# A two-layer hybrid decoder on one core: the query projections in another place in the order of work

## The chip, the core and the metric

The kernel runs on one core of a Trainium2 chip: TensorE (PE, matmuls), VectorE (DVE), ScalarE (ACT), GpSimd (POOL), and SyncE (SP), which issues all DMAs. The metric is the device time of one execution in microseconds (us); less is better.

## What is computed

Two layers over 512 prompt tokens and 64 sample tokens (8 sequences of 8) at width 1024. Each layer normalises the stream, projects it with one wide weight matrix, and runs two branches beside each other: retention (4 heads) and attention over the 128 (prompt) or 66 (sample) positions that an indexer scores highest. Both are gated, merged, projected out, and a gated per-layer input is added.

```python
def decoder_layer(x, p_i, pos, ret_s0, past, topk, ...):
    h = rmsnorm(x, g_norm)
    rq, rk, rv, rz, aq, ak, av, az, iq, ik, iw, gr, ga = in_projection(h, w_in, pos, q_gain, k_gain)
    o_r, s_new = retention(rq, rk, rv, ret_s0)
    u_r = einsum('bte,ed->btd', group_norm_heads(o_r) * silu(rz), w_o_ret)
    o_a = sparse_attention(aq, pos, k_all, v_all, iq, iw, ik_all, topk)
    u_a = einsum('bte,ed->btd', o_a * silu(az), w_o_att)
    m = sigmoid(gr) * u_r + sigmoid(ga) * u_a
    x = x + einsum('btd,de->bte', m, w_out)
    gate = sigmoid(einsum('btd,de->bte', x, w_ple_gate))
    return x + gate * einsum('btp,pd->btd', p_i, w_ple_proj), ak, av, ik, s_new
```

## The kernel before

Every float32 weight and activation is split into a high and a low part (`whi`/`wlo`, `xh`/`xl`), and each product is three matmuls (hi·hi, lo·hi, hi·lo). Weights arrive 1024 columns at a time in two staging buffers `wst`; `convert` makes the parts (ACT writes `whi`, DVE `wlo`).

The work is written as Python generators, one for each strand. A planner (`Streams.go`) keeps a model clock for each engine, estimates each operation's duration (`Op.dur`, by `_duration`), and issues next, again and again, the operation that could start first; priorities (`PRIO`) break ties. Its result is one fixed instruction order for each engine. On the chip each engine runs its own list strictly in order and waits where an operand is not there. Operations are all recorded by one helper, so the trace gives them all line L297; they are told apart by tiles.

The main strand of a layer walks through `PLAN`, a list of units, and issues their projections on PE. A unit of `proj_a` is 48 matmuls of 288 columns into PSUM banks `pm` (three of them); a unit of `proj_b` does five token tiles, 112 matmuls of 256 columns. Each finished bank is read out ("evacuated") by DVE and ACT:

- `kx`, `iq`: keys, values and indexer queries; `rv`: retention values; `az`: the attention branch's gate (`silz<-pm,R`).
- `aq0`, `aq1`: the attention queries, two groups of four heads (`aqx`). For each tile DVE scales (`misc<-pm,rcol,gqk`), normalises and rotates them in `misc` (three buffers `QQ`), PE transposes them (`ta<-cst,misc`), and ACT and DVE write them to `qs` (four slots `QS`; attention gives one back when it has finished a block and group).
- `rt h` stands for three units `rq`, `rk`, `rz` of retention head h, 0 to 3. `rq` and `rk` are rotated on the way out (`xl<-pm,rot`, `tb<-tb,rot`), `rz` is a gate (`silz<-pm,R`). Behind `rz` the strands `ret_p` (prompt) and `ret_s` (sample) of the head are started.
- `gr`, `ga` 0 to 7: 16 gate units (`misc<-pm,R`), spilled to DRAM.
- `wo`/`merge`, `wout`, `pp`, `wpg`: the output side. The first merge waits until all side strands have ended (`for e in sides`).

The side strands fill the engines beside the projections: `indexer` 1 to 3, one for each of the query blocks that need a selection (scores on PE, then 16 rounds of MAX8 and MATCH_REPLACE8 on DVE over 256, 384 and 512 columns of `xl`; lowest priority), `indexer_s`, `attend` (blocks j = 0 to 3, each with both query groups u, two key/value heads each, at most two pairs in flight), `attend_s`, `ret_p`, `ret_s`. Block j of `attend` waits for its indexer, and (j, u) for the queries of group u.

What sets the order here is the line `PLAN` and `Op.dur`:

```python
PLAN = _plan("kx iq rv0 rv1 az0 az1 az2 az3 aq0 aq1 rt0 rt1 rt2 rt3")
```

Of the kernel before, what the change touches and what calls it, by code (L numbers as in the profile page):

```python
# [105 lines left out]
class Op:  # L106
    __slots__ = ("eng", "fn", "a", "k", "name", "outs", "ins", "dur", "form")

    def __init__(self, eng, fn, name, a, k):
        self.eng, self.fn, self.name, self.a, self.k = eng, fn, name, a, k  # L110
        aps = [x for x in list(a) + list(k.values()) if isinstance(x, bass.AP)]
        out = k.get("out", a[0] if a else None)
        acc = k.get("accum_out")
        self.outs = [_box(x) for x in (out, acc) if x is not None]
        self.form = (_val(a[1].partition_size) > 64, min(2, _free(a[1]) - 1 >> 5)) if eng == "PE" else None
        self.ins = [_box(x) for x in aps if x is not out and x is not acc]
        self.dur = _duration(eng, name, out, aps, a, k)


def _val(x):  # L120
    return x() if callable(x) else x


def _box(ap):
    span = 1 + sum(s * (n - 1) for s, n in list(ap.ap)[1:])
    t = ap.tensor
    if ap.space in (bass.MemoryType.SB, PSUM):
        row = list(ap.ap)[0][0] or 1
        p0 = _val(ap.start_partition)
        c0 = ap.offset % row if row > 1 else 0  # L130
        return t.name, p0, p0 + _val(ap.partition_size), c0, c0 + span
    first = list(ap.ap)[0]
    return t.name, 0, 1, ap.offset, ap.offset + span + first[0] * (first[1] - 1)


def _free(ap):
    n = 1
    for s, c in list(ap.ap)[1:]:
        n *= c
    return n  # L140


def _duration(eng, name, out, aps, a, k):
    n = max(_free(x) for x in aps)
    psum = any(x.space == PSUM for x in aps[1:])
    if eng == "PE":
        if name == "transpose":
            return 0.110
        lhs = aps[1]
        if lhs.dtype == FT:  # L150
            if _free(lhs) <= 32:
                return 0.030 + n * 0.4e-3
            return 2 * max(0.11, n / 1.2e3 + 0.005)
        return max(0.108, (n + 32) / 2.4e3)
    if eng == "DVE":
        if name == "memset":
            return (n + 8) / 0.96e3
        ptr = sum(1 for x in aps[1:] if _free(x) == 1 and n > 4 and x.space != PSUM)
        if name in ("tensor_scalar", "tensor_copy") and not psum and all(x.dtype == FT for x in aps[:2]):
            return (n / 2 + 66) / 0.96e3 + 0.062 * min(ptr, 2)  # L160
        return (n + 64) / 0.96e3 + 0.062 * min(ptr, 2)
    if eng == "ACT":
        ptr = sum(1 for x in aps[1:] if _free(x) == 1 and n > 1)
        return (n + (61 if psum else 112)) / 1.2e3 + 0.093 * min(ptr, 2)
    if eng == "POOL":
        return 0.3 + (0.165 if k.get("op", a[-1]) == OP.pow else 0.0022) * n
    return {"page": 0.5, "gather": 0.74}.get(name, 0.47)
# [144 lines left out]
def tile_hybrid_decoder(ctx: ExitStack, tc: tile.TileContext, A, O):  # L312
# [96 lines left out]
    def plan(l):  # L409
# [6 lines left out]

        for st in PLAN:
            name, i = st[0], st[1:]
# [147 lines left out]
    def layer(l, xh, xl, kxb):  # L566
# [692 lines left out]
        la = None  # L1259
        for st in PLAN:  # L1260
            name, i = st[0], st[1:]
# [265 lines left out]
def _plan(order):  # L1527
    p = []
    for t in order.split():
        n, i = t[:2], t[2:]  # L1530
        p += [(n,)] if not i else [("rq", int(i)), ("rk", int(i)), ("rz", int(i))] if n == "rt" else [(n, int(i))]
    p += [(n, d) for d in range(KT) for n in ("gr", "ga")]
    for d in range(KT):
        p += [("wo", d), ("merge", d)]
    return p + [("wout", d) for d in range(KT)] + [("pp", 0), ("pp", 1)] + [("wpg", d) for d in range(KT)]


PLAN = _plan("kx iq rv0 rv1 az0 az1 az2 az3 aq0 aq1 rt0 rt1 rt2 rt3")
PAIRS_IN_FLIGHT = 2
PRIO = dict(convert=0, load=1, tables=6, indexer=7, indexer_s=3, attend=3, attend_s=5, ret_p=6, ret_s=4)  # L1540
NSLOT = dict(s4=3, qs=4, t2=5, pt=1, hi=3, lo=3)
# [82 lines left out]
```

## Time and profile before

| | us |
|---|---|
| median of 3 runs (lowest, highest) | 1159.26 (1154.34, 1162.0) |
| the profiled execution | 1155.49 |
| its span, first to last instruction | 1153.7 |

The profile is of one execution. PE's rows show a matmul's time in flight; matmuls overlap, so a busy PE is not a PE at its full rate. The stages below are cut where PE starts the first matmul of a unit: layer 0 has az at 77.0, aq0 at 103.8, rq0 at 153.1, rq2 at 203.8, gr0 at 280.7, the merge at 413.2; layer 1 has them at 646.1, 672.5, 720.6, 774.7, 850.8 and 983.5.

### The profile page before, as it was taken

The page shows a single profiled execution, that of the slowest core. Times are in us where ns is not written, and L with a number is a line of the kernel's source. Part 1 is how long each engine was busy: PE and PEld are TensorE (multiplying, and loading weights), DVE is VectorE, ACT ScalarE, POOL GpSimd, SP SyncE. Part 2 cuts the span into 40 slices and gives each one's busy share as a digit, 9 for nine tenths or more (in the row PEclk, how much of TensorE's full clock was granted, in tenths as well). Part 3 has the DMA queues.
Part 4 walks back from the last instruction along what each step waited for, and adds up shares of the span by engine and source line. Part 5 has one row for each costly group of instructions (what it writes and reads, how often), then busy time and mean ns, then how long its engine had stood idle before and what let it go on. Part 6 is the DMA issues. An engine that isn't in the chain of part 4 may idle for free.

```text
span 1153.7 us, 21594 instructions
## 1 busy us (share of the span) xinstructions
PE 1098.1 (95%) x8426; PEld 1058.7 (92%) x8426; DVE 764.6 (66%) x1979; ACT 525.7 (46%) x1116; POOL 57.3 (5%) x68
## 2 busy tenths in 40 slices
PE   8999789898999999999999996988999999999998
PEld 7989788797999999999999986987889999999998
DVE  6799999766654366443658999996576533764433
ACT  6732455554663343235446334565557533422331
POOL 0100110001000000000010011010000000000000
PEclk9999979999999999999999997998999999999999
DMA  6532112231333355523335111312323233655231
GB/s 194 153 113 74 37 55 83 86 115 53 97 107 115 125 192 157 184 87 109 105 113 168 63 56 37 111 38 94 113 74 107 88 114 125 203 168 163 80 122 47
DMA packets 53112, 124.80 MB, mean 108 GB/s; under 512 B 7442, under 2 KB 19602, under 8 KB 53010
## 3 DMA queue, kind: packets, MB, share of 16 engines
q1 hardware_dynamic: 53010, 123.42, 32.8%
q8 instruction: 66, 1.08, 0.4%
q14 instruction: 36, 0.29, 0.1%
HBM read 103.05 MB, written 20.35 MB: 107 GB/s over the span
## 4 chain that ended last, share of the span: by engine, by line
PE 65%; DVE 25%; ACT 4%; issue 3%; DMA 2%; SPq 1%; POOL 0%; DVEq 0%; ACTq 0%
PE pm L297 53%; DVE xl L297 7%; DVE sm L297 5%; DVE wlo L297 3%; PE acc L297 3%; PE oT L297 2%; PE tq L297 2%; PE tr L297 2%; DVE misc L297 2%; PE ta L297 2%; ACT tb L297 1%; DVE silz L297 1%; DVE t2k L297 1%; ACT whi L297 1%; DVE qs L297 1%
## 5 line engine op out<-in xcount | busy, mean ns | idle before, releaser
L297 PE MATMUL pm<-xh,whi 128*128 128x288 f32 x1536 | 460.0, 299 | 2.5 <-DVE misc L297 2.0
L297 PE MATMUL pm<-xh,wlo 128*128 128x288 f32 x1536 | 459.9, 299 | 0.0
L297 PE MATMUL pm<-xl,whi 128*128 128x288 f32 x1536 | 459.3, 299 | 0.0
L297 PEld LDWEIGHTS pm<-xh,whi 128*128 128x128 f32 x1536 | 292.0, 190 | 4.4 <-issue 1.8
L297 PEld LDWEIGHTS pm<-xl,whi 128*128 128x128 f32 x1536 | 292.3, 190 | 0.9 <-issue 0.4
L297 PEld LDWEIGHTS pm<-xh,wlo 128*128 128x128 f32 x1536 | 292.0, 190 | 1.1 <-issue 0.5
L297 ACT ACTIVATE whi<-wst 128x1024 fp32r<-128x1024 f32 (+4 forms) x148 | 150.1, 1016 | 218.3 <-PE pm L297 145.7
L297 DVE TENSOR_TENSOR wlo<-wst,whi 128x1024 fp32r<-128x1024 f32 (+4 forms) x148 | 173.0, 1171 | 87.0 <-ACT whi L297 86.9
L297 PE MATMUL pm<-whi,xh 128*128 128x256 f32 (+2 forms) x416 | 121.6, 298 | 9.7 <-DVE misc L297 9.7
L297 PE MATMUL pm<-wlo,xh 128*128 128x256 f32 (+2 forms) x416 | 120.3, 296 | 3.4 <-DVE wlo L297 3.4
L297 PEld LDWEIGHTS pm<-whi,xh 128*128 128x128 f32 x416 | 82.5, 198 | 11.4 <-ACT qs L297 10.5
L297 PE MATMUL pm<-whi,xl 128*128 128x256 f32 (+2 forms) x320 | 92.8, 290 | 0.0
L297 PEld LDWEIGHTS pm<-wlo,xh 128*128 128x128 f32 x416 | 82.5, 198 | 5.6 <-DVE wlo L297 4.6
L297 ACT ACTIVATE t2k<-t2k,sm 128x256 f32<-128x256 f32 (+3 forms) x111 | 64.7, 590 | 33.1 <-DVE sm L297 31.4
L297 DVE TENSOR_TENSOR misc<-pm,R 128x288 f32<-128x288 f32 x64 | 29.2, 456 | 64.3 <-PE pm L297 64.0
L297 PE MATMUL pm<-oh,whi 128*128 128x288 f32 x240 | 71.0, 296 | 0.0
L297 PE MATMUL pm<-oh,wlo 128*128 128x288 f32 x240 | 71.0, 296 | 0.0
L297 PE MATMUL pm<-ol,whi 128*128 128x288 f32 x240 | 70.9, 296 | 0.0
L297 PEld LDWEIGHTS pm<-whi,xl 128*128 128x128 f32 x320 | 62.0, 194 | 0.6 <-issue 0.4
L297 DVE MAX8 sm<-xl 128x8 f32<-128x256 f32 (+2 forms) x96 | 52.4, 551 | 0.8
L297 DVE MATCH_REPLACE8 xl<-sm,xl 128x384 f32<-128x384 f32 (+2 forms) x96 | 51.8, 541 | 0.0
L297 ACT ACTIVATE misc<-misc 128x288 f32<-128x288 f32 x64 | 27.9, 436 | 44.8 <-DVE misc L297 44.5
(258 smaller groups left out, 1712.0 us busy)
## 6 DMA issues: line engine op xcount, KB each, us to landing
wst<-in_wa SPq DMA_DIRECT2D x96, 512.0 KB, 3.6
wst<-in_wb SPq DMA_DIRECT2D x16, 512.0 KB, 3.9
wst<-in_wo SPq DMA_DIRECT2D x16, 512.0 KB, 3.8
zgr<-misc SPq DMA_DIRECT2D x16, 288.0 KB, 2.0
zga<-misc SPq DMA_DIRECT2D x16, 288.0 KB, 2.1
misc<-zgr SPq DMA_DIRECT2D x16, 288.0 KB, 2.8
misc<-zga SPq DMA_DIRECT2D x16, 288.0 KB, 4.6
s<-in_ckv SPq DMA_DIRECT2D x32, 128.0 KB, 3.2
```

Source lines behind the costliest of these rows:

```text
L297: op.fn(*op.a, **op.k)
```

## The change

Two edits. `PLAN` puts `aq0` behind retention head 0 and `aq1` behind head 1. And the planner takes a DVE or ACT operation to last 0.12 us longer where its output begins in another partition than its first input; this alters the order, not the operation. The operations and their number are the same.

```diff
         self.dur = _duration(eng, name, out, aps, a, k)
+        if eng in ("DVE", "ACT") and len(self.ins) and self.outs[0][1] != self.ins[0][1]:
+            self.dur += 0.12

-PLAN = _plan("kx iq rv0 rv1 az0 az1 az2 az3 aq0 aq1 rt0 rt1 rt2 rt3")
+PLAN = _plan("kx iq rv0 rv1 az0 az1 az2 az3 rt0 aq0 rt1 aq1 rt2 rt3")
```

The order on DVE in layer 0, from the last evacuation of az3 (`silz_400`) on. Before (lines are L297; L299 after the change):

```order
L297 MATCH_REPLACE xl<-sm_414,xl 128x384
L297 TENSOR_SCALAR xl<-xl 128x384
L297 TENSOR_TENSOR silz_400<-pm_68,R 128x288
L297 MAX sm_412<-xl 128x8
L297 TENSOR_TENSOR wlo_124<-wst_119,whi_121 128x1024
L297 SCALAR_TENSOR_TENSOR silz_400<-tb_434,silz_400 128x288
L297 MATCH_REPLACE xl<-sm_412,xl 128x384
L297 SCALAR_TENSOR_TENSOR misc<-pm_70,rcol,gqk 128x256
L297 TENSOR_REDUCE sm_416<-misc 128x4
```

After, at the same place:

```order
L299 MATCH_REPLACE xl<-sm_413,xl 128x384
L299 MAX sm_415<-xl 128x8
L299 TENSOR_TENSOR silz_400<-pm_68,R 128x288
L299 MAX sm_416<-xl 128x8
L299 TENSOR_TENSOR wlo_124<-wst_119,whi_121 128x1024
L299 SCALAR_TENSOR_TENSOR silz_400<-tb_434,silz_400 128x288
L299 MATCH_REPLACE xl<-sm_416,xl 128x384
L299 TENSOR_TENSOR xl<-pm_70,rot 128x288
L299 MAX sm_414<-xl 128x8
```

Behind az3 DVE used to scale and normalise queries (`misc`, `sm`); now it rotates retention head 0's queries (`xl<-pm_70,rot`). The indexer's rounds (MAX, MATCH_REPLACE) stand between in both.

The order on DVE in layer 0 around the sixteenth and last round of indexer 3 (MATCH_REPLACE over 512 columns). Before:

```order
L297 COPY qss<-ta_72 128x2x8x8
L297 TENSOR_TENSOR xl<-xl,tb_434 128x288
L297 TENSOR_TENSOR silz_399<-pm_68,R 128x288
L297 TENSOR_TENSOR t2k_429<-oT_73,t2k_429 64x256 x2
L297 TENSOR_TENSOR gs_437<-gs_437,cst 128x2
L297 MATCH_REPLACE xl<-sm_415,xl 128x512
L297 SCALAR_TENSOR_TENSOR silz_399<-tb_433,silz_399 128x288
L297 TENSOR_TENSOR qs_421<-ta_72,qs_421 64x2x128
L297 ISA t2k_427,sm_414<-tq_71,xl 128x256
L297 ISA sm_414 128x1
```

After:

```order
L299 MATCH_REPLACE xl<-sm_413,xl 128x512
L299 TENSOR_SCALAR rsm_129<-gs_438 128x4
L299 MAX sm_415<-xl 128x8
L299 TENSOR_TENSOR silz_399<-pm_70,R 128x288
L299 RECIPROCAL sm_416<-sm_416 128x1
L299 MATCH_REPLACE xl<-sm_415,xl 128x512
L299 TENSOR_TENSOR wlo_125<-wst_120,whi_122 128x1024
L299 SCALAR_TENSOR_TENSOR silz_399<-tb_434,silz_399 128x288
```

It stood between the two evacuations of rz1 (`silz_399`, head 1); now it stands behind the last evacuation of rz2 (head 2). From the first evacuation of az0 to the first of gr0 the list of DVE has 455 rows before and 440 after in layer 0, 451 and 443 in layer 1; the last round of indexer 3 is 301 and 360 rows into it in layer 0, 291 and 349 in layer 1.

The order on PE in layer 0 in the late gate units, around gr5. Before, where gr5 ends and ga5 begins:

```order
L297 MATMUL pm_69<-xh,whi_121 128x288
L297 MATMUL pm_69<-xl,whi_121 128x288
L297 MATMUL pm_69<-xh,wlo_124 128x288
L297 MATMUL pm_68<-xh,whi_122 128x288
L297 MATMUL pm_68<-xl,whi_122 128x288
L297 MATMUL pm_68<-xh,wlo_125 128x288
```

After, within gr5:

```order
L299 MATMUL pm_69<-xh,wlo_124 128x288
L299 MATMUL pm_69<-xh,whi_121 128x288
L299 MATMUL ta_72<-cst,t2k_428 128x128 x2
L299 MATMUL tq_71<-kdh,qs_420 128x512
L299 MATMUL tq_71<-kdl,qs_420 128x512
L299 MATMUL pm_69<-xl,whi_121 128x288
```

Rows of attention's block 3 (`tq`: scores, `ta`: transposes of the weights) now stand among the late gate units, which had projections alone. Matmuls and transposes of side strands that stand between the first row of az0 and gr0: 303 before, 255 after in layer 0, 298 and 243 in layer 1; among the gate units: 210 and 260, 214 and 270.

## Rows read from the trace of the kernel before

**Rows 1.** The page: busy time and share by engine, and the chain that ended last.

```profile
span 1153.7 us, 21594 instructions
...
PE 1098.1 (95%) x8426; PEld 1058.7 (92%) x8426; DVE 764.6 (66%) x1979; ACT 525.7 (46%) x1116; POOL 57.3 (5%) x68
...
PE 65%; DVE 25%; ACT 4%; issue 3%; DMA 2%; SPq 1%; POOL 0%; DVEq 0%; ACTq 0%
```

**Rows 2.** Busy time by stage; the first line names the columns.

```profile
core 0: us, PE busy (x) PEld busy (x) DVE busy (x) ACT busy (x) POOL busy (x), PEclk, DMA share, GB/s
77.00:103.80 26.80, 26.39 (x196) 25.67 (x195) 26.49 (x76) 8.81 (x15) 0.00 (x0) 1.00 0.24 80
103.80:153.10 49.30, 37.91 (x262) 35.06 (x261) 47.21 (x147) 21.60 (x47) 7.85 (x8) 0.87 0.17 55
153.10:203.80 50.70, 49.41 (x381) 47.71 (x382) 47.34 (x143) 27.48 (x64) 4.75 (x5) 0.96 0.21 73
203.80:280.70 76.90, 68.79 (x582) 63.17 (x581) 50.73 (x158) 42.73 (x109) 6.21 (x8) 0.98 0.26 85
280.70:413.20 132.50, 132.21 (x1046) 128.58 (x1046) 67.29 (x161) 64.58 (x135) 4.94 (x6) 1.00 0.34 114
413.20:578.90 165.70, 165.70 (x1250) 165.52 (x1249) 92.75 (x134) 63.63 (x102) 0.00 (x0) 1.00 0.42 135
646.10:672.50 26.40, 26.40 (x198) 26.22 (x197) 26.26 (x74) 9.56 (x19) 0.00 (x0) 1.00 0.27 88
672.50:720.60 48.10, 36.80 (x254) 34.12 (x252) 45.06 (x142) 18.98 (x44) 7.82 (x8) 0.86 0.12 40
720.60:774.70 54.10, 49.66 (x389) 47.00 (x390) 50.31 (x150) 29.81 (x69) 4.74 (x6) 1.00 0.24 79
774.70:850.80 76.10, 70.55 (x569) 63.16 (x568) 49.98 (x153) 40.73 (x102) 4.53 (x7) 0.93 0.27 89
850.80:983.50 132.70, 132.63 (x1054) 129.30 (x1053) 67.38 (x160) 66.00 (x139) 5.69 (x7) 1.00 0.33 111
983.50:1153.70 170.20, 165.93 (x1250) 165.51 (x1248) 85.63 (x136) 51.52 (x79) 0.00 (x0) 1.00 0.39 128
```

**Rows 3.** Groups of TensorE instructions, last eight gate units of layer 0 (362.2 to 413.2).

```profile
L297 PE MATMUL pm<-xl,whi 128*128 128x288 f32 x129 | 38.1, 296 | 0.0
L297 PE MATMUL pm<-xh,wlo 128*128 128x288 f32 x129 | 38.1, 296 | 0.0
L297 PE MATMUL pm<-xh,whi 128*128 128x288 f32 x128 | 37.9, 296 | 0.0
```

**Rows 4.** Waits of TensorE, 103.8 to 153.1: total us, times, longest.

```profile
PE pm L297 <- DVE misc L297: 5.0, 2, 3.1
PE ta L297 <- DVE qs L297: 2.2, 2, 1.3
```

**Rows 5.** Timeline of TensorE in the second query group: start, duration, instruction, [idle before].

```profile
140.60 0.28 PE L297 MATMUL pm<-wlo,xh 128*128 128x256 f32 x1
141.76 0.44 PE L297 MATMUL ta<-cst,misc 128*128 128x128 f32 x2 [0.88 <-DVE qs L297]
145.34 0.55 PE L297 MATMUL pm<-whi,xh 128*128 128x256 f32 x1 [3.14 <-DVE misc L297]
```

**Rows 6.** Groups of VectorE instructions, 103.8 to 153.1: busy us, mean ns.

```profile
L297 DVE MATCH_REPLACE8 xl<-sm,xl 128x384 f32<-128x384 f32 (+1 forms) x15 | 8.6, 576 | 0.0
L297 DVE MAX8 sm<-xl 128x8 f32<-128x384 f32 (+1 forms) x14 | 8.3, 590 | 0.1
```

**Rows 7.** Waits of TensorE, 203.8 to 280.7.

```profile
PE acc L297 <- ACT xh L297: 3.5, 3, 2.2
PE ta L297 <- ACT t2k L297: 3.1, 1, 3.1
```

**Rows 8.** Timeline: first score of query block 1, last attention product, layer 0.

```profile
182.23 0.39 PE L297 MATMUL tq<-kdh,qs 128*128 128x256 f32 x1 [0.38 <-DVE sm L297]
...
363.76 0.74 POOL L297 TENSOR_TENSOR silz<-xl,silz 128x256 f32<-128x256 f32 x1 [24.10 <-DVE xl L297]
```

## The prediction

> **What bounds the kernel now.** I read the page first, then a table of busy time cut at the units of the order of work, then the waits and the timeline of PE. The page calls PE 95% busy and DVE 66%, yet a quarter of the chain that ended last is DVE [rows 1]: these are averages over stages with different limits. The table [rows 2] shows them. From az0 to rq2 DVE is the bound: it is busy 26.49 of 26.80 us beside az, 47.21 of 49.30 beside the two query groups, 47.34 of 50.70 beside heads 0 and 1. From rq2 to gr0 it is busy 50.73 of 76.90 us and PE 68.79: neither is full, the two wait for each other. In the gate units DVE has half its time free (67.29 of 132.50), and from the merge on PE is busy without a gap (165.70 of 165.70). Layer 1 repeats this row for row.
>
> PE's own need is less than the stages take. Eight gate units without side work are 386 matmuls in 51.0 us [rows 3], 0.132 us each, so a unit of 48 takes 6.34 us. The query stage of layer 0 is 224 projection matmuls and 38 others (262 [rows 2]); at 0.132 that is 34.6 us, and it took 49.3. The waits that carry the difference end with DVE's `misc` and `qs` [rows 4], that is with the scaling and the transposed copies of queries. The timeline [rows 5] shows how: transposes of queries wait 0.88 us for `qs`, and the next tile then waits 3.14 us for a bank that DVE has not read, because its list holds both the queries' chain and the indexer's rounds (29 MAX8 and MATCH_REPLACE8 in this stage, 16.9 us [rows 6]). PE stood at a granted clock of 0.87 here.
>
> **The change part by part.** Nothing is added or removed; the 0.12 us exists in the planner alone and costs nothing on the chip but the order it makes. What moves is which work shares a stage. The three units of head 0 now come between az3 and aq0, those of head 1 between aq0 and aq1. Beside the two query groups DVE had 47.2 - 16.9 = 30.3 us of work other than the indexer's rounds, in long chains for each tile, next to PE's 34.6; three retention units now come between the two bursts. The rounds, which only fill, spread over more units, and the last one comes behind rz2 instead of within rz1, as the order shows. The weight loads of the moved units move with them on SP's queue, as do the loads of the retention states, which now come sooner; the DMA engines are 16 to 26% busy in these stages [rows 2], so I take that at nothing. If that cover failed, a 512 KB load would show as a wait for `wlo`, and none is among the long waits of the query stage [rows 4].
>
> Term A, from az0 to gr0. DVE's work there was 171.8 us in layer 0 and 171.6 in layer 1 (sums of four rows each [rows 2]). Its list from the first az evacuation to the first gate evacuation shrinks from 455 rows to 440 and from 451 to 443; at the mean duration of a row that leaves 166.1 and 168.6 us. Of these rows 360 and 349 come up to the last round of the indexer: 135.9 and 132.8 us of work. As long as the indexer has rounds left I let DVE be as busy as in the three DVE-bound stages of before, 121.0 of 126.8 us and 121.6 of 128.6, or 95.5% and 94.6%: 142.4 and 140.4 us. What is left then is rq3, rk3 and rz3, in layer 1 half of rz2 too, with side work as dense as from rq2 to gr0 before (97 and 90 side rows in three units, 194 and 187 in six); a unit took 76.9 / 6 = 12.8 and 76.1 / 6 = 12.7 us there, so 38.4 and 44.4 us. Together 180.8 and 184.8 us instead of 203.7 and 204.7 [rows 2]: **22.9 and 19.9 us gained**.
>
> Term B, the gate units. Attention runs later against the projections, and what it did not do before gr0 it does here: 50 and 56 more side rows on PE. The 16 units alone are 101.5 us, so 210 side rows cost 31.0 of the 132.5 us in layer 0 and 214 cost 31.2 of 132.7 in layer 1 [rows 2, 3], 0.148 and 0.146 us a row with their waits: **7.4 and 8.2 us lost**.
>
> Behind the merge nothing moves. The sum is 42.8 - 15.6 = 27.2 us, from the profiled execution's 1155.5 us (1.8 above its span [rows 1]) to 1128.3. The median of the runs lies 3.8 us above that execution; I forecast 1130.
>
> The bounds: at DVE's share beside az alone (26.49 of 26.80) the filled part of A falls by 4.9 and 6.3 us, and at PE's bare 0.132 us a row B falls by 0.8 each, which gives 1115.5. If instead DVE keeps its share over the whole stretch, 171.8 of 203.7 and 171.6 of 204.7, A is only 6.7 and 3.5 us and the sum 1160.9. I stay near the former because heads 0 and 1 were already worked through beside the indexer's rounds at 47.34 of 50.70 us, with the same mixture that now fills the longer stretch.
>
> Is there so much to gain on PE at all? PE's busy time leaves 203.7 - 182.5 = 21.2 us idle from az0 to gr0 in layer 0; the weight loads (PEld) leave 203.7 - 171.6 = 32.1 [rows 2]. The Trainium skill's "Perfetto Trace Analysis", section "Identifying the Most-Contended Engine", says that matmul busy time is a poor measure of headroom and weight-load busy time a good one. By the first, term A in layer 0 would be capped at 21.2 us and the sum at 1130.0; by the second no cap is touched. The trace sides with the page: the gate units' matmuls last 296 ns in flight and follow each other at 132 [rows 3].
>
> **The rivals.** *The waits come along.* Retention and sample attention stall PE by latency, not by DVE's load: 3.5 us for ACT's `xh` and 3.1 in one wait for `t2k` [rows 7]. If heads 0 and 1 bring such waits into the filled stretch, DVE starves too, and its overall share holds: 1150 to 1161, within 1%. Against it, heads 0 and 1 stood beside the indexer before. Chance 0.16.
>
> *The end of attention becomes the bound* (the slower side). The merge waits for all side strands. In layer 0, block 1's first score starts at 182.23 and the last product ends at 364.5 [rows 8], a chain of 182.3 us with 48.7 to spare before 413.2. Now that score stands in rk2, 315 DVE rows behind the first az evacuation: 315 x 0.3775 / 0.955 = 124.6, so about 201.6; the same chain ends at 383.9, and the gates at 77.0 + 180.8 + 139.9 = 397.7. The order agrees that little is spare: block 3 stands among gr5. Up to 196 us of chain it costs nothing; each us beyond is lost. With 20% more (218.8) 22.7 us are lost in layer 0, and as much again in layer 1: 1174. Against it, the chain will share DVE with fewer rounds than before. Chance 0.09.
>
> *PE's clock.* The granted clock was 0.87 and 0.86 in the query stages, between its levels of 1.2 and 2.4 GHz, behind waits such as the 3.14 us one [rows 5], and 1.00 beside az, where DVE was just as full [rows 2]. If PE stood at 0.87 through 142 us, 18.5 us of full-rate time would be lost there against 8.4 in the same work before; DVE's bound hides little more than that, and 10 us a layer would take the sum to 1148. The skill's "TensorE: Matmul & The Clock Gate", section "A second HAM failure mode: psum-queue depth-cycling", says that short idle spells between groups that cycle through PSUM banks make the clock oscillate, which is this case's three `pm` banks. The 0.96 from rq0 to rq2, with such groups throughout, speaks against it [rows 2]. Chance 0.07.
>
> *More.* The last units before gr0 are no slower than those of heads 0 and 1 were (50.7 / 6 = 8.5 us, 54.1 / 6 = 9.0): 12.9 and 12.8 us less, 1103. Chance 0.07. That the order would not change is excluded by the order itself.
>
> **How the numbers follow.** The forecast, 1130 with its own range 1113 to 1147, has 0.61. Two runs of this kernel differ by up to 0.7%, so about 1% is what a measurement can tell. Faster by over 1% is below 1147.7: the forecast, the deep case, and half of the clock's, 0.71; within 1%: the waits and the other half, 0.20; slower 0.09. The range 1108 to 1152 leaves out the slow case, the deep one and a quarter of the waits', 0.20 in all.
>
> **What would show it.** Right: from az0 to gr0 some 181 to 185 us with DVE over 90% busy until the last 512-column round; waits of `pm` for `misc` in the query stages below 1 us each instead of 3.1; gate units some 7 us longer in each layer; nothing changed behind the merge. Wrong: DVE at 85% in the filled stretch (waits for `tr`, `acc`, `gs`), PE waiting on `ta` or `oT` in the last gate units, or a granted clock below 0.9 in more stages than before.

## The result and the profile after

The changed kernel takes 1114.54 us (median of 4 runs, 1112.86 to 1117.67) beside 1160.63 for the kernel before in the same session (4 runs, 1154.34 to 1163.09): a ratio of 0.961, with a 95% interval of 0.957 to 0.966. The forecast was 1130 with a range of 1108 to 1152. Each ratio here is to the kernel before in the same session, whose median lay between 1154.5 and 1160.6, so two changed versions are compared by their own times. The profiled execution took 1115.49 us, 40.0 less than the profiled one of before. From its page, the span, the busy time by engine and the chain that ended last:

```profile
span 1113.7 us, 21594 instructions
...
PE 1084.8 (97%) x8426; PEld 1049.9 (94%) x8426; DVE 759.1 (68%) x1979; ACT 525.2 (47%) x1116; POOL 57.4 (5%) x68
...
PE 63%; DVE 28%; ACT 3%; issue 2%; DMA 1%; SPq 1%; POOL 0%; DVEq 0%; ACTq 0%
```

The instruction counts are those of [rows 1]; PE's matmul time fell by 13.3 us, DVE's by 5.5. The page by itself doesn't say where 40 us went, the stages do. This is the table of busy time cut at az0, rq3 (219.5 and 769.0; the last round of indexer 3 ends at 222.4 and 768.6), gr0 and the merge; columns as in [rows 2]:

```profile
76.00:219.50 143.50, 138.26 (x1074) 132.18 (x1073) 138.85 (x426) 67.20 (x153) 14.19 (x15) 0.99 0.24 79
76.00:255.80 179.80, 173.56 (x1352) 164.18 (x1351) 167.32 (x514) 89.83 (x210) 17.35 (x19) 0.98 0.25 81
219.50:255.80 36.30, 35.30 (x281) 32.00 (x280) 28.46 (x90) 22.63 (x57) 3.16 (x4) 0.95 0.29 91
255.80:392.50 136.70, 136.70 (x1114) 132.26 (x1113) 71.36 (x173) 74.92 (x161) 5.67 (x7) 1.00 0.33 113
392.50:558.20 165.70, 165.70 (x1250) 165.52 (x1249) 92.69 (x134) 63.67 (x102) 0.00 (x0) 1.00 0.41 135
...
623.40:803.80 180.40, 170.97 (x1332) 161.42 (x1331) 164.29 (x499) 88.87 (x206) 18.08 (x19) 0.98 0.24 80
769.00:803.80 34.80, 33.24 (x267) 30.42 (x266) 25.56 (x75) 22.56 (x58) 3.18 (x4) 0.95 0.24 85
803.80:943.50 139.70, 138.81 (x1131) 134.10 (x1130) 72.29 (x182) 75.47 (x164) 5.66 (x7) 1.00 0.33 112
943.50:1113.70 170.20, 165.89 (x1249) 165.47 (x1248) 85.62 (x136) 51.50 (x79) 0.00 (x0) 1.00 0.39 128
```

| stage | before | after | measured | forecast |
|---|---|---|---|---|
| up to az0, layer 0 | 77.0 | 76.0 | -1.0 | 0 |
| az0 to gr0, layer 0 | 203.7 | 179.8 | -23.9 | -22.9 |
| gate units, layer 0 | 132.5 | 136.7 | +4.2 | +7.4 |
| merge to az0 of layer 1 | 232.9 | 230.9 | -2.0 | 0 |
| az0 to gr0, layer 1 | 204.7 | 180.4 | -24.3 | -19.9 |
| gate units, layer 1 | 132.7 | 139.7 | +7.0 | +8.2 |
| merge to the end | 170.2 | 170.2 | 0 | 0 |
| sum | | | -40.0 | -27.2 |

The same stretch before, az0 to gr0 in each layer, as one row:

```profile
77.00:280.70 203.70, 182.50 (x1417) 171.61 (x1416) 171.78 (x520) 100.62 (x235) 18.81 (x20) 0.95 0.22 74
646.10:850.80 204.70, 183.42 (x1406) 170.50 (x1405) 171.63 (x516) 99.08 (x231) 17.09 (x20) 0.94 0.23 75
```

Three things moved. PE's idle time from az0 to gr0 (length less PE busy) fell from 21.2 and 21.3 us to 6.2 and 9.4. PE's granted clock there rose from 0.95 and 0.94 to 0.98. And 68 and 77 more PE records, those of the side strands, stand in the gate units (1114 and 1131 beside 1046 and 1054 in [rows 2]). PE's waits between rq0 and rq2 (104.5 to 192.5: heads 0 and 1 and both query groups; total us, times, longest):

```profile
PE tr L299 <- DVE xh L299: 3.1, 1, 3.1
PE tr L299 <- DVE iqs L299: 1.2, 2, 0.9
PE acc L299 <- ACT xh L299: 0.3, 1, 0.3
```

and from rq2 to gr0 (192.5 to 255.8):

```profile
PE acc L299 <- ACT xh L299: 1.0, 1, 1.0
PE ta L299 <- ACT t2k L299: 0.3, 1, 0.3
```

No bank `pm` is waited for any more, where DVE's `misc` cost 5.0 us [rows 4]; and the latencies of retention and of sample attention, 3.5 and 3.1 us in the last six units [rows 7], are 1.0 and 0.3. One wait is new, 3.1 us of `tr` for DVE's `xh`, within the first query group. From az0 to gr0 the waits of PE that the profile lists add up to 20.8 us before and 6.1 after in layer 0, 21.2 and 9.3 in layer 1. In layer 1 `pm` for `misc` went too (6.2 us), but `acc` for `xh` didn't shrink: 1.4 us before, 2.9 after.

### The profile page after: what moved, and what is told of

It is laid out like the page before. It is cut to its first block, busy times and chain, and to the rows that moved or that the text cites. A ratio compares the mean times of both kernels' runs of the same rounds, so it can differ in the third digit from the quotient of the medians.

```text
span 1113.7 us, 21594 instructions
## 1 busy us (share of the span) xinstructions
PE 1084.8 (97%) x8426; PEld 1049.9 (94%) x8426; DVE 759.1 (68%) x1979; ACT 525.2 (47%) x1116; POOL 57.4 (5%) x68
## 4 chain that ended last, share of the span: by engine, by line
PE 63%; DVE 28%; ACT 3%; issue 2%; DMA 1%; SPq 1%; POOL 0%; DVEq 0%; ACTq 0%
PE pm L299 53%; DVE xl L299 7%; DVE sm L299 5%; DVE wlo L299 5%; PE oT L299 3%; PE tq L299 3%; PE acc L299 2%; DVE misc L299 2%; DVE silz L299 2%; PE ta L299 2%; PE tr L299 1%; DVE t2k L299 1%; DVE iqs L299 1%; DVE tb L299 1%; DVE qs L299 1%
## 5 line engine op out<-in xcount | busy, mean ns | idle before, releaser
L299 PE MATMUL pm<-xh,whi 128*128 128x288 f32 x1536 | 458.2, 298 | 0.0
L299 PE MATMUL pm<-xl,whi 128*128 128x288 f32 x1536 | 457.1, 298 | 0.0
L299 PE MATMUL pm<-xh,wlo 128*128 128x288 f32 x1536 | 456.8, 297 | 0.0
L299 PEld LDWEIGHTS pm<-xl,whi 128*128 128x128 f32 x1536 | 290.4, 189 | 1.6 <-issue 0.5
L299 PEld LDWEIGHTS pm<-xh,whi 128*128 128x128 f32 x1536 | 290.1, 189 | 0.9
L299 PEld LDWEIGHTS pm<-xh,wlo 128*128 128x128 f32 x1536 | 290.0, 189 | 0.8
L299 ACT ACTIVATE whi<-wst 128x1024 fp32r<-128x1024 f32 (+4 forms) x148 | 150.1, 1016 | 200.3 <-PE pm L299 128.6
L299 DVE TENSOR_TENSOR wlo<-wst,whi 128x1024 fp32r<-128x1024 f32 (+4 forms) x148 | 172.8, 1169 | 82.0 <-ACT whi L299 81.6
L299 PE MATMUL pm<-wlo,xh 128*128 128x256 f32 (+2 forms) x416 | 117.5, 290 | 1.9 <-DVE wlo L299 1.9
L299 PE MATMUL pm<-whi,xh 128*128 128x256 f32 (+2 forms) x416 | 118.2, 291 | 0.0
L299 PE MATMUL pm<-whi,xl 128*128 128x256 f32 (+2 forms) x320 | 93.0, 291 | 0.0
L299 PEld LDWEIGHTS pm<-wlo,xh 128*128 128x128 f32 x416 | 80.1, 193 | 3.5 <-DVE wlo L299 2.4
L299 PEld LDWEIGHTS pm<-whi,xh 128*128 128x128 f32 x416 | 80.1, 193 | 0.7 <-issue 0.4
L299 PE MATMUL pm<-oh,whi 128*128 128x288 f32 x240 | 70.9, 296 | 0.0
L299 PE MATMUL pm<-oh,wlo 128*128 128x288 f32 x240 | 70.9, 295 | 0.0
L299 PE MATMUL pm<-ol,whi 128*128 128x288 f32 x240 | 70.8, 295 | 0.0
L299 ACT ACTIVATE t2k<-t2k,sm 128x256 f32<-128x256 f32 (+3 forms) x102 | 58.7, 583 | 25.2 <-DVE sm L299 21.0
L299 PEld LDWEIGHTS pm<-whi,xl 128*128 128x128 f32 x320 | 61.6, 193 | 0.5 <-issue 0.4
L299 DVE TENSOR_TENSOR misc<-pm,R 128x288 f32<-128x288 f32 x64 | 29.1, 454 | 41.9 <-PE pm L299 41.5
L299 DVE MAX8 sm<-xl 128x8 f32<-128x256 f32 (+2 forms) x96 | 52.4, 549 | 0.8
L299 DVE MATCH_REPLACE8 xl<-sm,xl 128x256 f32<-128x256 f32 (+2 forms) x96 | 51.7, 540 | 0.0
L299 DVE TENSOR_TENSOR ptl<-ta,pth 128x512 fp32r<-128x512 f32 (+1 forms) x48 | 28.7, 598 | 29.8 <-ACT pth L299 29.6
```

Source lines behind the costliest of these rows:

```text
L299: op.fn(*op.a, **op.k)
```

## The experiments

Four explanations were set against each other, and the expectations call them by letters or by what they say. **A**, the prediction's: DVE's total work is the bound until the indexer's last round. **B**: the two bursts of query work, one behind the other, outrun DVE, and parting them is what helps. **C**: what the change moves is the side strands: the retention strands of heads 0 and 1 start earlier, under the indexer's rounds, and attention slides later, to where PE has projections to cover its latencies. **D** came last: gr0 may not start before every query tile stands in `qs`. In the two expectations on the strands the letters stand for halves of C: C there is earlier retention alone, D is later attention alone. Only in the two five-slot runs is D the wait of gr0.

**The two edits apart.** The changed kernel without the planner's 0.12 us, and the kernel before with it alone:

```diff
-            self.dur += 0.12        (with its condition; new PLAN kept)
```

> The new order of units without the planner's extra 0.12 us. Theory (the two bursts of query work on VectorE, parted by the units of heads 0 and 1, let the indexer's rounds fill): nearly all of the gain, 0.96 to 0.975 of before, az to gr0 180 to 186 us in each layer instead of 203.7 and 204.7. Rival (the planner's better estimate keeps TensorE from standing at the head of its list for operands that are late): little of the gain, 0.985 to 1.00.

```diff
+            self.dur += 0.12        (with its condition; old PLAN kept)
```

> The planner's extra 0.12 us with the old order of units. Theory of the bursts: az to gr0 stays at 200 to 206 us, the ratio 0.99 to 1.005. Rival (the estimate does it): 0.965 to 0.98.

Measured: 1116.97 us, 0.965 (0.961 to 0.970), for the table of units alone, and 1146.43, 0.991 (0.988 to 0.995), for the 0.12 us alone. `PLAN` does nearly all of it; the 0.12 us, worth 8.0 us by itself, adds some 2.4 to it, with runs that overlap. The 0.12 us alone puts az0 at 75.3 instead of 77.0, and with the new `PLAN` at 76.0 instead of 77.4; from the merge to az0 of layer 1 it makes 231.6 us of 232.9, and 230.9 of 232.8. So the 3.0 us that the table above has ahead of az0 in the two layers are its work. I had costed it at nothing but the order it makes, and hadn't counted that order ahead of az0.

**The bursts.** Both groups behind head 1, still one behind the other; and the first group ahead of head 0, the second behind it:

```diff
-PLAN = _plan("... az3 rt0 aq0 rt1 aq1 rt2 rt3")
+PLAN = _plan("... az3 rt0 rt1 aq0 aq1 rt2 rt3")
```

> Both query groups behind heads 0 and 1 (rt0 rt1 aq0 aq1 rt2 rt3), with the 0.12 us. Theory of the bursts: the two groups stand together again, so the second takes about 30 us and waits of pm for misc come back; ratio 0.975 to 0.995. Rival (it is enough that the retention starts sooner and fills TensorE): ratio 0.955 to 0.97, as with the change. Rival (four qs slots): waits as before, since block 0 frees them no sooner.

```diff
+PLAN = _plan("... az3 aq0 rt0 aq1 rt1 rt2 rt3")
```

> The groups parted, but each ahead of its head (aq0 rt0 aq1 rt1 rt2 rt3), with the 0.12 us. Theory of the bursts: parting them is what counts, so 0.955 to 0.975. Rival (it is the place behind the first retention head, where the indexer has fewer rounds left): 0.98 to 1.00.

Measured: 1119.41 us, 0.967 (0.963 to 0.972), and 1117.84, 0.966 (0.961 to 0.970). Together behind head 1, the second group's unit is as slow as ever (34.4 us in layer 0, where it was 32.0 before), and yet the kernel gains all but a few us: what gets shorter are the units from rq2 to rz3, 57 us instead of 76.9. B's sign, waits of `pm` for `misc`, did not come back: from aq0 to rq2 there is none, and the longest wait is 3.3 us of `ta` for `qs`. B falls. The other run shows that one head ahead of the second group is enough for most of the gain.

**DVE's load.** Eight rounds instead of sixteen in indexer 3, in the kernel before and in the changed one:

```diff
-            yield from topk(s, 128, TOPK_P)
+            yield from topk(s, 128, TOPK_P if j < 3 else TOPK_P // 2)
```

> The kernel before with 8 rounds instead of 16 in indexer 3 (it leaves half of that block's selection out). That takes 8 x (0.68 + 0.68) = 10.9 us of VectorE's work out of each layer. Theory A (from az on VectorE's total work is the bound as long as rounds are left, whatever its order): the stretch az to gr0 falls by 8 to 11 us a layer, the time by 16 to 22 us, ratio 0.981 to 0.986. Theory B (TensorE loses its time to the burst of the second query group alone): the burst stays, under 8 us in all, ratio above 0.993.

> The changed kernel with the same 8 rounds left out of indexer 3. Theory A: VectorE is 96% busy up to the last round, so 16 to 22 us less than the changed kernel, ratio to before 0.943 to 0.949. Theory B: the bursts are gone, the rounds fill idle time only: within 8 us of the changed kernel, ratio to before above 0.955.

Measured: 1140.19 us, 0.986 (0.981 to 0.991), from the kernel before, and 1114.52, 0.964 (0.959 to 0.968), from the changed one, which is no gain over the changed kernel's own 0.961. The stages of the second, az0 to gr0 and gate units, layer by layer:

```profile
76.00:256.40 180.40, 172.94 (x1387) 164.66 (x1386) 161.13 (x498) 92.42 (x218) 18.82 (x20) 0.99 0.25 84
256.40:391.80 135.40, 135.17 (x1081) 130.55 (x1080) 69.96 (x165) 71.50 (x153) 4.66 (x6) 1.00 0.33 111
622.70:804.40 181.70, 172.99 (x1382) 163.91 (x1381) 159.07 (x491) 91.59 (x214) 20.16 (x20) 0.99 0.25 83
804.40:938.80 134.40, 134.40 (x1080) 130.76 (x1079) 69.43 (x168) 72.57 (x155) 5.58 (x6) 1.00 0.33 111
```

DVE has 6.2 and 5.2 us less to do there than in the changed kernel, and the stretch is 0.6 and 1.3 us longer. So in the changed kernel DVE's total doesn't set it, and A's 16 to 22 us didn't come. (The profiled execution, 1110.8 us, is 4.7 shorter than that of the changed kernel; the gate units have it, 1.3 and 5.3.) What the freed time bought is side work done sooner: 35 and 50 more PE records ahead of gr0.

The kernel before answered otherwise. Its time fell by 14.5 us (18.6 between profiled executions), to 0.986, the edge of A's range (0.981 to 0.986) and outside B's (above 0.993). But the time went where A had not put it:

```profile
76.50:277.80 201.30, 186.59 (x1478) 174.18 (x1477) 166.33 (x508) 103.95 (x244) 19.27 (x20) 0.97 0.24 80
277.80:404.80 127.00, 126.33 (x984) 123.57 (x983) 63.39 (x150) 61.49 (x127) 4.94 (x6) 1.00 0.32 109
638.40:840.60 202.20, 186.89 (x1502) 174.45 (x1500) 166.60 (x514) 105.37 (x251) 18.84 (x21) 0.97 0.24 80
840.60:964.90 124.30, 124.30 (x959) 122.19 (x958) 61.64 (x139) 59.80 (x120) 3.92 (x5) 1.00 0.33 111
```

The stretch fell by 2.4 and 2.5 us, where A had 8 to 11, and the gate units by 5.5 and 8.4, since 61 and 96 more PE records stood ahead of gr0. So the rounds did cost the kernel before time, and cost the changed one none that can be measured. As the account of what sets the length of the changed stretch, A falls. (Half the rounds also came with a granted clock of 0.97 where it was 0.95 and 0.94, so a part of the 14.5 us can be the clock's; no run separates it.)

**The strands.** In the changed kernel, retention strands held back until the second query group is issued; in the kernel before, attention held back until head 0's gate is issued:

```diff
+        def late(gen):
+            yield e_late                  # set behind aq1
+            yield from gen
-                    side(ret_p(h, t), PRIO["ret_p"])
-                    side(ret_s(h, t), PRIO["ret_s"])
+                    side(late(ret_p(h, t)), PRIO["ret_p"])
+                    side(late(ret_s(h, t)), PRIO["ret_s"])
```

> The changed kernel, but the side strands of retention heads 0 and 1 may start only when the second query group has been issued. Theory C (the gain comes from retention's side strands running beside the indexer's rounds instead of in the slow units behind them): most of the gain is lost, 20 to 35 us slower than the changed kernel, ratio to before 0.98 to 1.0. Theory D (it comes from attention being pushed into the gate units): 0 to 8 us slower, ratio 0.96 to 0.97.

```diff
         def attend():
             yield e_k
+            yield e_late                  # set behind rz of head 0
```

> The kernel before, but attention may start only when the three units of retention head 0 have been issued (some 23 us later). Theory D: block 1 and what follows slide towards the gate units as with the change, so half or more of the gain: ratio 0.965 to 0.98. Theory C: retention stays where it was, nothing gained; the second query group even waits longer for qs slots: ratio 0.995 to 1.02.

Measured: 1133.84 us, 0.980 (0.976 to 0.985), so about half of the gain is lost; and 1140.58, 0.985 (0.980 to 0.990), so over a third of it is there without any unit moved. Neither expectation came out whole: 19.3 us slower than the changed kernel is just short of the first one's C (20 to 35) and far from its D, and 0.985 lies between the second one's two. Late retention, az0 to gr0 of both layers and between them one unit, rk2 of layer 0:

```profile
75.40:262.70 187.30, 175.34 (x1376) 162.83 (x1375) 168.34 (x510) 93.32 (x216) 17.77 (x19) 0.98 0.23 78
187.00:211.20 24.20, 19.55 (x132) 15.52 (x132) 20.48 (x70) 12.88 (x35) 3.07 (x3) 0.86 0.08 25
631.70:819.00 187.30, 173.90 (x1365) 162.73 (x1364) 164.73 (x502) 91.74 (x214) 18.32 (x19) 0.97 0.23 77
```

The query groups themselves are quicker than in the changed kernel (17.3 and 16.4 us beside 22.9 and 20.3), but the strands of two heads then meet in rk2, which takes 24.2 us for 48 projection matmuls. The whole loss, 7.5 and 6.9 us, stands from az0 to gr0. Late attention in the kernel before, the four stages:

```profile
76.70:266.50 189.80, 175.28 (x1375) 163.58 (x1374) 165.30 (x507) 91.95 (x215) 17.83 (x19) 0.98 0.24 77
266.50:404.40 137.90, 137.06 (x1088) 133.08 (x1087) 72.74 (x177) 72.48 (x155) 5.66 (x7) 1.00 0.33 113
637.50:820.10 182.60, 167.47 (x1271) 158.86 (x1270) 161.07 (x480) 86.27 (x198) 17.45 (x18) 0.97 0.23 77
820.10:969.20 149.10, 147.30 (x1190) 140.93 (x1189) 77.65 (x198) 78.09 (x172) 6.38 (x8) 0.98 0.32 108
```

The stretch ahead of gr0 is 13.9 and 22.1 us shorter, the gate units 5.4 and 16.4 longer. And the second query group, 32.0 us in the kernel before, takes 18.2 with the first still right ahead of it: it was slow because attention ran inside it, not because of the first group. The two runs each take one half of the change away or give it. Their effects, 14.5 us lost and 14.3 gained between profiled executions (19.3 and 14.1 by medians), would leave some 11 of the 40 to the 0.12 us and to what the two do together, if they add, which no run tests. Late retention also makes a jam of its own in rk2, so not all of its loss need be what the earlier start had gained. C stands in that both halves count; their shares stay open.

**How far it goes.** The second group one head later still:

```diff
-PLAN = _plan("... az3 rt0 aq0 rt1 aq1 rt2 rt3")
+PLAN = _plan("... az3 rt0 aq0 rt1 rt2 aq1 rt3")
```

> The changed kernel with its second query group one head later still: PLAN ends rt0 aq0 rt1 rt2 aq1 rt3. It tests the rival of the forecast, that the end of attention becomes the bound. In the changed kernel head 2 takes 27 us from rq2 (192.5) to rq3 (219.5) in layer 0 and 29 us in layer 1, and the last product of attention ends at 377.4, 15 us before the merge at 392.5. If the chain behind the second group has no slack within it, it ends some 27 us later, 12 us behind the present merge in each layer: about 1139, with PE waiting before the merge. If the chain gets shorter where it runs beside gate units alone, as theory C has it (attention later is better, since PE never waits there), nothing is lost: 1110 to 1118. If all that counts is that retention's strands start early, also no loss and no gain: 1113 to 1118.

Measured: 1140.01 us, 0.985 (0.982 to 0.989). As slow as the first case said, but for another reason: PE waits nowhere between gr0 and the merge, in either layer. The time goes between rz3's last projection and gr0's first, here from 249.3 and from 809.2 us on, each with the stretch ahead of it:

```profile
76.40:249.30 172.90, 164.75 (x1303) 158.01 (x1301) 159.99 (x488) 80.05 (x183) 17.71 (x18) 0.99 0.26 85
249.30:271.80 22.50, 17.21 (x112) 11.54 (x110) 13.38 (x46) 14.11 (x37) 1.48 (x3) 0.77 0.12 41
...
634.90:809.20 174.30, 164.11 (x1281) 157.11 (x1280) 155.11 (x471) 79.65 (x181) 16.71 (x17) 0.97 0.25 80
809.20:834.90 25.70, 20.83 (x119) 14.00 (x118) 16.12 (x58) 12.43 (x34) 3.16 (x4) 0.64 0.20 65
```

For 22.5 and 25.7 us PE's list holds side strands alone. The code says why: the main strand takes the gates' buffers out of `misc` and first waits for every query tile (`for e in list(e_q.values()) + ...: yield e`, ahead of gr0). There are eight tiles and four slots `qs`; the eighth gets the slot that attention gives back at the end of block 1. ACT's write of it, first in the changed kernel and then here:

```profile
251.02 0.38 ACT L299 ACTIVATE qs<-ta 64x256 fp32r<-64x256 f32 x1
```

```profile
271.31 0.38 ACT L299 ACTIVATE qs<-ta 64x256 fp32r<-64x256 f32 x1
```

In the changed kernel it comes 4.8 us ahead of gr0 (255.8); here gr0 starts at 271.8. The next two runs tested this, with a fifth slot (and one buffer `t2` less, to fit) in this kernel and in the changed one:

```diff
-NSLOT = dict(s4=3, qs=4, t2=5, pt=1, hi=3, lo=3)
+NSLOT = dict(s4=3, qs=5, t2=4, pt=1, hi=3, lo=3)
```

> The kernel with the second query group behind head 2 (PLAN ends rt0 aq0 rt1 rt2 aq1 rt3), with five qs slots instead of four and, so that it fits, four t2 buffers instead of five. With four slots that kernel ran no projection on PE from 249.3 to 271.8 us in layer 0 and from 809.2 to 834.9 in layer 1. Theory D: the code lets gr0 start only when every query tile stands in qs; the eighth tile waits for the fourth slot that attention gives back, that is for the end of block 1 (written from 271.3 us on), while the seventh, which waits for the third, was written from 254.3 us on. With five slots the eighth tile needs the third, so gr0 comes at about 255 to 257, some 15 us sooner in layer 0, and as much in layer 1, of which the four t2 buffers may take a few us: 1108 to 1118 instead of 1140.0. If instead gr0 is held back because the side strands have the higher priority, or because the fourth t2 buffer is the limit, the gap stays: 1135 to 1145.

> The changed kernel with five qs slots and four t2 buffers. There the last query tile is written at 251.0 us in layer 0, 4.8 us ahead of gr0 at 255.8, so by theory D the slot count does not hold the gate units back and the time stays within 1% of the changed kernel: 1108 to 1122. If waits for qs slots in the two query groups (22.9 and 20.3 us in layer 0) were still costing projections, they would shorten by several us each: 1098 to 1107. If the four t2 buffers starve attention, it is slower: 1125 or more.

Measured: 1134.82 us, 0.981 (0.976 to 0.987), and 1116.15, 0.964 (0.959 to 0.969). The mechanism of D is right, since gr0 came at 255.8 instead of 271.8 and 21.2 us sooner in layer 1; the time forecast from it (1108 to 1118) is wrong, and by its time alone the run would look like the rival's 1135 to 1145. What stood before gr0 went behind it, and there the next limit waited: the gate units take 144.3 and 147.3 us beside 136.7 and 139.7 in the changed kernel, and 3.5 and 2.5 us more are lost behind the merge (granted clock 0.72 in its first 9.9 us in layer 0). Layer 0 of the five-slot kernel with the group behind head 2, az0 to gr0, the gate units up to 390, and the last 10 us ahead of the merge at 400.1:

```profile
75.70:255.80 180.10, 169.25 (x1325) 160.13 (x1324) 164.29 (x493) 84.76 (x193) 18.20 (x18) 0.98 0.25 85
255.80:390.00 134.20, 132.88 (x1086) 128.59 (x1085) 70.10 (x186) 74.91 (x167) 5.65 (x7) 1.00 0.30 102
390.00:400.10 10.10, 6.76 (x54) 6.56 (x52) 4.62 (x8) 4.50 (x9) 0.19 (x1) 0.94 0.61 209
```

Its last product of attention on POOL, and the first matmul of the merge on PE, which waits for the copies made from it:

```profile
399.91 0.73 POOL L299 TENSOR_TENSOR silz<-t2k,silz 128x256 f32<-128x256 f32 x1 [25.71 <-DVE t2k L299]
```

```profile
400.13 0.61 PE L299 MATMUL pm<-oh,whi 128*128 128x288 f32 x1 [3.37 <-ACT oh L299]
```

This is the prediction's slower rival, the end of attention, at work. In the changed kernel a fifth slot changes nothing that can be measured, as D has it.

**A search for more.** az0 and az1 ahead of the retention values, in the changed kernel:

```diff
+PLAN = _plan("kx iq az0 rv0 az1 rv1 az2 az3 rt0 aq0 rt1 aq1 rt2 rt3")
```

> The changed kernel with az0 and az1 ahead of the two retention-value units: PLAN begins kx iq az0 rv0 az1 rv1 az2 az3. It looks for a version that beats both. The rounds of the indexers begin behind iq in either order. If what limits the stretch from az0 to gr0 is latency of side work beside too little projection work, it gains nothing here, since the same units stand behind az3: 1112 to 1118. If the first rounds are what holds az up (26.49 of 26.80 us of DVE in the kernel before), two of the four az units beside rv units, which DVE reads out more cheaply, gain 2 to 4 us a layer: 1107 to 1111.

Measured: 1126.63 us, 0.975 (0.972 to 0.978), slower than the changed kernel; both expectations missed. Layer 0 has a gap like that of D again, 252.4 to 270.8 with no projection on PE (the last write of a query tile ends at 269.4); in layer 1, without the gap, iq to the merge takes 366.4 us beside 367.8 in the changed kernel. No version beat the changed one.

## Why the prediction was right, and where it was not

**The forecast's case came true, on a step that failed.** From az0 to gr0 the terms were -22.9 and -19.9, measured -23.9 and -24.3, DVE's work was 167.3 and 164.3 us, forecast at 166.1 and 168.6, and its share up to the last round was to be 95.5 and 94.6%. It was 96.8 and 95.3%:

```profile
76.00:222.40 146.40, 141.16 (x1096) 135.08 (x1095) 141.75 (x437) 69.42 (x158) 15.20 (x16) 0.99 0.24 81
623.40:768.60 145.20, 137.32 (x1065) 130.59 (x1063) 138.33 (x422) 66.24 (x148) 14.90 (x15) 0.99 0.23 78
```

All this fits term A, which took the length of the filled part to be DVE's work over its share, and still that step is wrong: with 6.2 us of DVE's work taken out, the changed stretch didn't shorten. That the term came out so close is in part luck, since its two parts missed and offset each other: 146.4 and 145.2 us up to the last round, forecast at 142.4 and 140.4, and 33.4 and 35.2 behind it, forecast at 38.4 and 44.4. A list that also holds work that only fills (the rounds) keeps an engine looking full: with half the rounds, DVE was 96.9% busy up to the last one again (98.19 of 101.30 us in layer 0).

What the rows allow in its place: PE takes 0.144 us a record from az0 to gr0 before (203.7 by 1417), 0.133 after, 0.130 with half the rounds, and 0.132 in bare gate units [rows 3]. After the change PE runs at about the pace of projections alone; before, waits kept it above. (The records are of several widths, so the paces compare roughly.) The largest of these waits was `pm` for `misc`, 5.5 and 6.2 us, which half the rounds left at 5.6 and 6.2; retention's and attention's latencies made up much of the rest in layer 0. The two runs on the strands show that their places count. That PE alone bounds the stretch now is a reading, since no run took work from PE.

**PE's clock**, which the sum left out, has a share in the gain that no run separates from the waits. Between levels of 1.2 and 2.4 GHz, a mean of 0.95 and 0.94 over the stretch is some 20 and 25 us at the lower one, and 0.98 some 7. At a granted clock of 0.50 (before, 145.9 to 147.8) a 256-column matmul followed the last at 0.21 us, at 1.00 (115.1 to 117.2) at 0.12. If PE had worked through all of the time at the lower level, about half of it would be lost; so, as an estimate from these rows, the clock's own share is at most 7 of the 23.9 us and 9 of the 24.3.

**Layer 1** gained 4.4 us more than its term: 9.2 behind the last round, less 4.8 up to it. The pace behind it was mis-sized: three units at that of the slow ones of before (12.7 us each) are 38.1 us, and rq3 to gr0 took 34.8.

**The gate units** lost 4.2 and 7.0 us instead of 7.4 and 8.2. The price of 0.148 and 0.146 us a side row was that of the waits and rows of before; for the 50 and 56 rows that came in it was 4.2 / 50 = 0.084 and 7.0 / 56 = 0.125, less than the 0.132 of the lower bound. (A row of the order can stand for two or more PE records: the 50 and 56 rows are the 68 and 77 records above.)

**Ahead of az0** 3.0 us were gained that the sum had at nothing, through the 0.12 us.

Together 1.0 + 4.4 + 3.2 + 1.2 + 3.0 are the 12.8 us between the sum's 27.2 and the 40.0. One slip in the bounds: with DVE's share beside az, 26.49 of 26.80, layer 1 falls by 6.0 us and not 6.3, so the lower bound is 1115.8.

**What would show it.** Waits of `pm` for `misc` below 1 us: there are none. Nothing changed behind the merge: 165.7 and 170.2 as before. Granted clock: 0.99 up to the last round, where the clock's rival wanted 0.87. Of the waits, one came along, the 3.1 us of `tr` for `xh`, in a first query group of 22.9 us that took 17.3 with retention held back; DVE did not starve by it, so the rival's case did not come. The stretch came out just under its 181 to 185 us.

**The headroom.** PE's busy time left 21.2 us in layer 0, and 23.9 were gained, which looks like a verdict for weight loads as the measure. It is not one: 65 records left the stretch, and PE's busy time fell from 182.5 to 173.6. The idle time itself went from 21.2 to 6.2. Of the rule in the Trainium skill's "Perfetto Trace Analysis", section "Identifying the Most-Contended Engine", this run shows neither side.

**The end of attention** was rightly priced as a rival and rightly left out. The first score of block 1 and the last product, layer 0, as [rows 8]:

```profile
207.68 0.28 PE L299 MATMUL tq<-kdh,qs 128*128 128x256 f32 x1
```

```profile
376.69 0.75 POOL L299 TENSOR_TENSOR silz<-t2k,silz 128x256 f32<-128x256 f32 x1 [25.71 <-DVE t2k L299]
```

The score came 6 us later than worked out (201.6), and 15.1 us are spare before the merge, where 13.8 were forecast. The score at 182.23 in [rows 8] is not block 1's first but its second (block 0 has the eight ahead of these two). The first, in the same timeline, is

```profile
179.37 0.28 PE L297 MATMUL tq<-kdh,qs 128*128 128x256 f32 x1
```

So the chain was 185.1 us before, not 182.3, and took 169.8 after. The prediction missed the nearer limit, the wait of gr0 for the last query tile: 4.8 us ahead. It stands in a line of the code beside the change, and a wait inside a planner leaves no wait in a trace.

## What to carry to other kernels

A busy share doesn't say whether an engine is the bound if part of its work only fills. The same rounds taken out gave 14.5 us before the change and none after it, with DVE 95.5 and 96.8% busy beside them: take some of that work out before you build a sum on it. When units are reordered, ask for each side strand where it will now run, and move those with long latencies to where the critical engine has plain work of its own. Then look for what ends that freedom: slots given back late and events that the next stage waits for, which show in the trace only as a stretch without main work.

## What was not expected of the hardware

PE's granted clock fell where its list held side strands' short matmuls alone, though it had work: 0.77 and 0.64 in the 22.5 and 25.7 us without projections (PE 17.21 and 20.83 us busy, with gaps of up to 1.4 us), after 0.99 and 0.97 in the stretches ahead of them. The two levels are 1.2 and 2.4 GHz, so about half of the first stretch and 0.7 of the second ran at the lower. The 22.5 and 25.7 us hold what that cost; no run separates it from the gaps.
